# Deferred split subtracts, a LayerNorm scaled by VectorE, later triangle transposes and a merge that starts with two blocks by channels, in a hybrid gMLP, S5 and attention block

## The chip, the cores and the metric

One core of one Trainium2 chip runs the whole block in one launch. The metric is the device time of one execution in microseconds. Engines are called as the profile calls them: PE is TensorE, DVE VectorE, ACT ScalarE, POOL GpSimd, SP the engine that issues most loads.

## The reference

One decoder layer on x of shape (1024, 1024) in float32, with three sub-layers, each between RMSNorms. The part around the change is the first one:

```python
h = rms_norm(x, g_mix_pre)
z_gm, z_s5, z_ga, z_gb = split(h @ w_in)                 # 2048, 512, 1024, 1024 columns
u, v = split(gelu(z_gm))
v = layer_norm(v, ln_g, ln_b)
sv = einsum('gts,bnsgc->bntgc', tril(w_s), v) + b_s      # 8 chunks of 128 positions, 8 channel groups of 128
y_gm = u * sv
y_s5 = s5(z_s5);  y_s5 = y_s5 * sigmoid(y_s5 @ w_glu)    # 512 channels
merged = sigmoid(z_ga) * (y_gm @ w_br_gm) + sigmoid(z_gb) * (y_s5 @ w_br_s5)
x = x + rms_norm(merged @ w_mix_out, g_mix_post)
```

Cross-attention into a memory of 256 positions and a SwiGLU feed-forward layer follow; the change does not touch them.

## The kernel before, in words

**Float32 products from three fast ones.** Every large product is made of operands that are split in two float32r tiles, a high and a low half: `put` (line 527) copies the source to the high half on ScalarE (line 529) and subtracts that from the source on VectorE (line 530). Weights are split the same way by `split` (lines 103 and 104), from a raw tile that SP has loaded (line 94). `mm3` issues three matmuls, high by high, high by low and low by high (all appear at line 519). `tblock` (line 539) makes one 128x512 tile in a PSUM bank, over n channel groups, three products each. There are 8 PSUM banks of 128x512, 38 slots of 128x1024 in SBUF, 8 buffers of split weights and 3 of raw weights.

**Order.** The program is recorded in a fixed order; each engine and each DMA queue works through its instructions in the order in which they are recorded. Side work is written as generators that are put in a queue (`bg`); `sub()` (line 67), called after every second channel group of the main products (6 matmuls), advances each generator that is due and then splits at most one weight tile ahead. A generator's `yield n` puts it off for n calls of `sub`. So the place of a side step among the matmuls is set by these counts. A weight tile is split ahead only while fewer than 7 of the 8 split buffers are in use and at most 3 tiles ahead; `rel` gives buffers back. A raw weight load stands in SP's queue behind the subtract of an earlier split, whose buffer it takes, and the other loads of SP behind it.

**The stages around the change**, in this order:

1. `v_phase` (line 1146) makes v in two halves of four 128x1024 tiles, from products in the four banks X and the four banks Y. For one half of the positions, `ln` (line 1153) gets the mean from sums that the GELUs accumulated, the variance from squares on ScalarE (line 1160), then a reciprocal root in ten small VectorE operations (`rms_slow`), and normalizes: one small VectorE product for the bias (line 1164) and one ScalarE activation with scale and bias for each of four tiles (line 1167). `ln(1)` runs beside the product "21" into Y; after it come the adds that empty Y (line 1247) and their GELUs, and then the product "T4" into X, whose GELUs (line 1255) are followed by `ln(0)`. The generator `wturn` (line 1218), put in the queue ahead of "T4", transposes the triangular position weights on TensorE (line 1223), in two groups of four tiles, copies them out on ScalarE (line 1224), and adds to the bias tile a product with the LayerNorm's bias (lines 1230 and 1231), again in two groups. The first transposes take the first bank that line 1247 has emptied.
2. `s5_out` (line 1060) makes the GLU: for each of 4 channel blocks m and each half of the positions, 12 matmuls, a sigmoid on ScalarE (line 1076), a multiply on VectorE (line 1077) and the split `put` (line 1078). The next product, with `w_br_s5`, needs all four blocks as channels: its first two output blocks are made as four tiles, over channels 0 to 2 first and then over channel 3; the other six follow with `tblock`. Each tile is multiplied out of PSUM by the gate `gb` on VectorE and stored by ScalarE's DMA queue (`mb`).
3. `gm_gen` (line 1259) runs as side work among these products, the gating: for each of 8 channel groups and each half, four matmuls of v with the triangle into one bank, `scalar_tensor_tensor` out of PSUM (line 1282, seen at line 140), a multiply by u (line 1284, seen at line 134) and `put` (line 1285), one half at every second `sub`. u is loaded by SP one group ahead (line 1267).
4. `merge` (line 1291) drains the side work, then makes eight output blocks of two halves each: 24 matmuls over the eight channel groups with `w_br_gm`, multiplied by `ga` (line 1311), added to `mb` (line 1312) and split. `ga` and `mb` of the next block are loaded ahead (lines 1297 and 1298).

Of the kernel before, what the change touches and what calls it, by code (L numbers as in the profile page):

```python
# [9 lines left out]
F = mybir.dt.float32  # L10
# [26 lines left out]
class Builder:  # L37
# [1022 lines left out]
    def s5_out(self):  # L1060
        nc = self.nc
        while len(self.yT) < 4 or not self.yok:
            self.sub()
        yT, self.yT = self.yT, None
        yr, self.yr = self.yr, None
        ys = []
        for m in range(4):
            if m % 2 == 0:
                w = self.get(("glu", m // 2))
            y = self.pair()  # L1070
            t = self.slot()
            for half in range(2):
                o = slice(half * 512, half * 512 + 512)
                ps = self.bank()
                self.tblock(ps, w, (m % 2) * 128, lambda k: tuple(s[:, o] for s in yT[k]), 4)
                nc.scalar.activation(out=t[:, o], in_=ps, func=AF.Sigmoid)  # L1076
                self.tt(t[:, o], t[:, o], yr[m][:, o], ALU.mult)
                self.put(tuple(s[:, o] for s in y), t[:, o])
            ys.append(y)
            if m % 2:  # L1080
                self.rel()
        yT = yr = None
        gb = {}

        def lg(m):
            gb[m] = self.slot()
            nc.sync.dma_start(gb[m], self.gd["gb"][m])
        lg(0)
        lg(1)
        self.bg(self.gm_gen(), 3)  # L1090
        late = []
        w = self.get(("bs", 0))

        tiles = [(m, half, self.bank()) for m in range(2) for half in range(2)]
        for ks in (range(3), range(3, 4)):
            for m, half, ps in tiles:
                for k in ks:
                    self.mm3(ps, tuple(x[:, k, m * 128:m * 128 + 128] for x in w),
                             tuple(s[:, half * 512:half * 512 + 512] for s in ys[k]), k == 0, k == 3)
                self.sub()  # L1100
                if ks[0]:
                    o = slice(half * 512, half * 512 + 512)
                    self.tt(gb[m][:, o], ps, gb[m][:, o], ALU.mult)
        tiles = ps = None
        self.rel()
        late += [(self.gd["mb"][m], gb.pop(m)) for m in range(2)]
        lg(2)
        for m in range(2, 8):
            if m < 7:
                lg(m + 1)  # L1110
            if m % 2 == 0:
                w = self.get(("bs", m // 2))
            g = gb.pop(m)
            for half in range(2):
                o = slice(half * 512, half * 512 + 512)
                ps = self.bank()
                self.tblock(ps, w, (m % 2) * 128, lambda k: tuple(s[:, o] for s in ys[k]), 4)
                self.tt(g[:, o], ps, g[:, o], ALU.mult)
            if m % 2:
                self.rel()  # L1120
            while late:
                nc.scalar.dma_start(*late.pop(0))
            late.append((self.gd["mb"][m], g))
        nc.scalar.dma_start(*late.pop(0))
# [21 lines left out]
    def v_phase(self, fin):  # L1146
# [6 lines left out]
        def ln(half):  # L1153
            st = sums[half]
            mu = st[:, 40:44]
            self.tt(mu, st[:, 32:36], st[:, 36:40], ALU.add)
            self.ts(mu, mu, -1.0 / D, ALU.mult)
            for t in range(4):
                j = self.jk.tile([P, 1024], BF, name="jk", tag="jk", bufs=1)
                nc.scalar.activation(out=j, in_=vt[4 * half + t], func=AF.Square, bias=mu[:, t:t + 1],  # L1160
                                     accum_out=st[:, t:t + 1])
                yield 1
            yield from self.rms_slow(st, 4)
            self.tt(st[:, 48:52], mu, st[:, 16:20], ALU.mult)
            for t in range(4):
                v = vt[4 * half + t]
                nc.scalar.activation(out=v, in_=v, func=AF.Identity, scale=st[:, 16 + t:17 + t], bias=st[:, 48 + t:49 + t])  # L1167
                if t % 2:
                    yield 1
            if not half:  # L1170
                self.vok = True
# [75 lines left out]
            self.tt(vt[t][:, h0], Y[t], vt[t][:, h0], ALU.add)  # L1247
            gelu(vt[t][:, h0], vt[t][:, h0], st(0, 0, t))
        Y = None
        self.bg(wturn(), 2)  # L1250
        run(X, "T4", False)
        del self.fxs["T4"]
        self.hT = None
# [5 lines left out]
    def gm_gen(self):  # L1259
        nc, i = self.nc, self.ins  # L1260
        self.ygm = [None] * 8
        us = {}

        def lu(g):
            if g < 8:
                us[g] = self.slot()
                nc.sync.dma_start(us[g], self.ud[g])
        lu(0)
        while not self.vok:
            self.sub()  # L1270
        for g in range(8):
            y = self.pair()
            lu(g + 1)
            u = us.pop(g)
            for half in range(2):
                o = slice(half * 512, half * 512 + 512)
                ps = self.bank()
                for n in range(4):
                    self.mm(ps[:, n * 128:n * 128 + 128], self.vt[4 * half + n][:, g * 128:g * 128 + 128],
                            self.wt[:, g * 128:g * 128 + 128], True, True)  # L1280
                t = self.tmp()
                self.stt(t.rearrange("p (n t) -> p n t", n=4), ps.rearrange("p (n t) -> p n t", n=4), self.gc[:, 32 + g:33 + g],
                         self.bb[:, g * 128:g * 128 + 128].unsqueeze(1).to_broadcast([P, 4, 128]), ALU.mult, ALU.add)
                self.tt(u[:, o], t, u[:, o], ALU.mult)
                self.put(tuple(s[:, o] for s in y), u[:, o])
                yield 2
            self.ygm[g] = y
            u = y = t = ps = None
        self.vt = self.bb = None

    def merge(self):
# [3 lines left out]
        def lg(m):  # L1295
            ld[m] = (self.slot(), self.slot())
            nc.sync.dma_start(ld[m][0], self.gd["ga"][m])
            nc.sync.dma_start(ld[m][1], self.gd["mb"][m])
        self.drain()
        lg(0)  # L1300
        self.mg = self.halves()
        for m in range(8):
            if m < 7:
                lg(m + 1)
            w = self.get(("a", m))
            g, b = ld.pop(m)
            for half in range(2):
                o = slice(half * 512, half * 512 + 512)
                ps = self.bank()
                self.tblock(ps, w, 0, lambda k: tuple(s[:, o] for s in self.ygm[k]))  # L1310
                self.tt(g[:, o], ps, g[:, o], ALU.mult)
                self.tt(g[:, o], g[:, o], b[:, o], ALU.add)
                self.put(self.hv(self.mg, half, m, True), g[:, o])
                if half:
                    self.rel()
        self.ygm = self.wt = None
# [647 lines left out]
```

## Time and profile before

| | |
|---|---|
| median of 3 runs | 1670.89 us (1670.71 to 1671.16) |
| the profiled execution's own time | 1670.15 us |
| its span, first to last instruction | 1668.4 us |
| TensorE busy, mean granted clock | 1628.1 us (98%), 0.994 |
| VectorE, ScalarE busy | 1150.6 us (69%), 681.7 us (41%) |

Times in the profile count from the span's start. A row's line number is often that of a helper: 519 is every split product, 134, 140 and 146 are the VectorE helpers `tt`, `stt` and two-operation `ts`, 144 is `ts` with one operation, 529 and 530 are `put`. Matmul ends are modelled, and a few matmul records can be missing, so counts of a stretch can be one or two short.

### The profile page before, as it was taken

What the parts mean: (1) busy time and instruction counts of PE and PEld (TensorE: products, weight loads), DVE (VectorE), ACT (ScalarE), POOL (GpSimd) and SP (SyncE); (2) the same over time, 40 slices, a digit from 0 to 9 for tenths busy, and PEclk for the clock granted to TensorE, in tenths of its full rate; (3) what the DMA queues carried; (4) which work ended last, traced back from release to release, by engine and by line L of the source; (5) the groups of instructions that cost most, each with busy time, mean ns of one, the idle gap of its engine ahead of it and who ended that gap; (6) DMA issues with size and microseconds to landing.
All of it is one profiled execution on the core that took longest, in us unless ns stands there. A gap on an engine that the chain in (4) does not pass through costs nothing.

```text
span 1668.4 us, 20995 instructions
## 1 busy us (share of the span) xinstructions
PE 1628.1 (98%) x7788; PEld 1364.4 (82%) x7788; DVE 1150.6 (69%) x2053; ACT 681.7 (41%) x1196; POOL 102.7 (6%) x97
## 2 busy tenths in 40 slices
PE   7999989999999999999999999999999999999997
PEld 7898878887887778888888888888888888888886
DVE  5679788967444674447864577687778777666778
ACT  6642212135457222235543447753233223245454
POOL 0025500012500000000000000000000000000000
PEclk9999999999999999999999999999999999999999
DMA  8669922245231474444523153673545446463634
GB/s 278 207 122 200 234 74 90 76 134 186 113 113 51 163 283 158 141 147 143 172 69 125 53 192 112 216 244 130 180 139 173 149 158 202 142 225 132 226 112 161
DMA packets 223414, 259.53 MB, mean 156 GB/s; under 512 B 14824, under 2 KB 157200, under 8 KB 223120
## 3 DMA queue, kind: packets, MB, share of 16 engines
q1 hardware_dynamic: 176208, 181.24, 33.7%
q10 hardware_dynamic: 26496, 60.18, 9.7%
q0 software_dynamic: 20608, 16.78, 5.9%
q8 instruction: 61, 1.00, 0.2%
q14 instruction: 41, 0.34, 0.1%
HBM read 183.31 MB, written 77.33 MB: 156 GB/s over the span
## 4 chain that ended last, share of the span: by engine, by line
PE 83%; DVE 7%; ACT 5%; issue 2%; DMA 2%; SPq 0%; ACTq 0%; DVEq 0%
PE ps L519 79%; DVE act L134 2%; DVE ws L104 1%; ACT jk L575 1%; DVE ws L134 1%; ACT ws L103 1%; DMA wr<-in_ca_w_kv_dram 1%; ACT act L529 1%; DVE act L530 1%; DVE act L140 1%; PE ps L587 1%; ACT jk L1160 1%; DMA wr<-actd 1%; PE ps L508 1%; ACT act L1167 0%
## 5 line engine op out<-in xcount | busy, mean ns | idle before, releaser
L519 PE MATMUL ps<-act,ws 128*128 128x512 f32 (+1 forms) x4212 | 970.1, 388 | 9.6 <-ACT act L529 7.3
L519 PEld LDWEIGHTS ps<-act,ws 128*128 128x128 f32 x4212 | 775.4, 189 | 165.9 <-ACT act L529 8.1
L519 PE MATMUL ps<-ws,act 128*128 128x512 f32 x1392 | 332.8, 395 | 0.0
L519 PEld LDWEIGHTS ps<-ws,act 128*128 128x128 f32 x1392 | 270.2, 208 | 45.0
L134 DVE TENSOR_TENSOR act<-act 128x512 f32<-128x512 f32 (+6 forms) x521 | 287.3, 580 | 15.2 <-ACT act L1076 8.0
L519 PE MATMUL ps<-ws 128*128 128x512 f32 x852 | 193.3, 389 | 0.0
L519 PEld LDWEIGHTS ps<-ws 128*128 128x128 f32 x852 | 159.9, 188 | 33.2
L104 DVE TENSOR_TENSOR ws<-wr,ws 128x1024 fp32r<-128x1024 f32 x100 | 122.1, 1223 | 93.3 <-ACT ws L103 93.1
L134 DVE TENSOR_TENSOR act<-ps,act 128x512 f32<-128x512 f32 x201 | 135.6, 683 | 43.5 <-PE ps L519 34.1
L134 DVE TENSOR_TENSOR ws<-act,ws 128x512 fp32r<-128x512 f32 x107 | 74.0, 692 | 88.9 <-ACT ws L1754 51.8
L134 DVE TENSOR_TENSOR ws<-tm,ws 128x512 fp32r<-128x512 f32 x108 | 78.2, 724 | 79.4 <-ACT ws L1547 58.9
L1547 ACT CAST ws<-tm 128x512 fp32r<-128x512 f32 x88 | 54.8, 622 | 168.8 <-PE ps L519 111.5
L103 ACT CAST ws<-wr 128x1024 fp32r<-128x1024 f32 x100 | 104.7, 1047 | 42.8 <-PE ps L519 29.3
L134 DVE TENSOR_TENSOR ws<-wr,ws 128x512 fp32r<-128x512 f32 x130 | 91.7, 706 | 28.2 <-ACT ws L1547 14.9
L529 ACT CAST act<-act 128x512 fp32r<-128x512 f32 (+1 forms) x92 | 57.5, 637 | 129.5 <-DVE act L134 117.1
L530 DVE TENSOR_TENSOR act<-act 128x512 fp32r<-128x512 f32 (+1 forms) x92 | 65.3, 720 | 46.1 <-ACT act L529 46.1
L519 PE MATMUL ps<-act 128*128 128x256 f32 (+2 forms) x504 | 86.6, 317 | 0.2
L519 PEld LDWEIGHTS ps<-act 128*128 128x128 f32 x504 | 74.7, 190 | 9.6 <-DVE act L134 0.8
L1754 ACT CAST ws<-act 128x512 fp32r<-128x512 f32 x71 | 44.2, 622 | 89.6 <-PE ps L519 48.3
L1831 POOL DMA_DIRECT2D out_dram<-act x4 | 2.2, 561 | 1171.8 <-DVE act L134 1171.8
L530 DVE TENSOR_TENSOR act<-ps,act 128x512 fp32r<-128x512 f32 x48 | 32.5, 687 | 39.7 <-ACT act L529 39.7
L890 ACT ACTIVATE act<-ps 128x512 f32<-128x512 f32 x32 | 19.2, 600 | 80.4 <-PE ps L519 46.6
(164 smaller groups left out, 1112.5 us busy)
## 6 DMA issues: line engine op xcount, KB each, us to landing
wr<-in_ffn_w_gu_dram SPq DMA_DIRECT2D x39, 512.0 KB, 4.2
actd<-act ACTq DMA_DIRECT2D x77, 256.0 KB, 2.2
wr<-actd SPq DMA_DIRECT2D x38, 512.0 KB, 3.7
wr<-in_w_in_dram SPq DMA_DIRECT2D x28, 512.0 KB, 3.9
act<-in_ffn_w_gu_dram SPq DMA_DIRECT2D x22, 512.0 KB, 5.1
act<-in_ffn_w_down_dram SPq DMA_DIRECT2D x44, 256.0 KB, 4.3
td<-act POOLq DMA_DIRECT2D x40, 256.0 KB, 6.6
pd<-act ACTq DMA_DIRECT2D x17, 512.0 KB, 4.4
```

Source lines behind the costliest of these rows:

```text
L103: self.nc.scalar.copy(hi, t)
L104: self.nc.vector.tensor_tensor(out=lo, in0=t, in1=hi.bitcast(F), op=ALU.subtract)
L134: self.nc.vector.tensor_tensor(out=out, in0=a, in1=b, op=op)
L140: self.nc.vector.scalar_tensor_tensor(out=out, in0=a, scalar=s, in1=b, op0=op0, op1=op1)
L508: nc.tensor.matmul(py[:, o], self.rr[:, 512 + i * 128:640 + i * 128], cc[:, 512 + i * 128:640 + i * 128], start=False, stop=True)
L519: self.nc.tensor.matmul(ps, a, b, start=start, stop=stop, skip_group_check=more)
L529: self.nc.scalar.copy(dst[0], src)
L530: self.nc.vector.tensor_tensor(out=dst[1], in0=src, in1=dst[0].bitcast(F), op=ALU.subtract)
L575: self.nc.scalar.activation(out=j[:, 0:n], in_=src, func=AF.Square, accum_out=col)
L890: nc.scalar.activation(out=g[:, half * 512:half * 512 + 512], in_=ps, func=AF.Sigmoid)
L1547: self.nc.scalar.copy(t[:, 0:512], now)
L1754: nc.scalar.copy(w[:, h[0]], src)
```

## The change

It has four parts.

- In `s5_out` and in `gm_gen` the split's ScalarE copy is recorded where it was, and its VectorE subtract one half later: behind the multiply of the next half, the last one after the loop (`rest`).
- In `ln` the four normalizations of a half are done by VectorE, one `tensor_scalar` each with two scalars from a statistics tile: add the negative mean, multiply by the reciprocal root. The small product for the bias is gone.
- `wturn` is put in the queue with a delay of 5 instead of 2, so all its four steps come three calls of `sub` later.
- In `merge` the first two blocks are made as four tiles, over channel groups 0 to 5 first, then over groups 6 and 7 of each; `ga` and `mb` of blocks 0 and 1 are loaded at the start, those of block 2 after these tiles, and the split weights of both blocks are given back after them. Blocks 2 to 7 are as before.

```diff
@@ s5_out
+                nc.scalar.copy(y[0][:, o], t[:, o])
+                if rest:
+                    self.tt(*rest, ALU.subtract)
+                rest = y[1][:, o], t[:, o], y[0][:, o].bitcast(F)
-                self.put(tuple(s[:, o] for s in y), t[:, o])
...
+        self.tt(*rest, ALU.subtract)
@@ v_phase, ln
-            self.tt(st[:, 48:52], mu, st[:, 16:20], ALU.mult)
             for t in range(4):
                 v = vt[4 * half + t]
-                nc.scalar.activation(out=v, in_=v, func=AF.Identity, scale=st[:, 16 + t:17 + t], bias=st[:, 48 + t:49 + t])
+                self.ts(v, v, st[:, 40 + t:41 + t], ALU.add, st[:, 16 + t:17 + t], ALU.mult)
@@ v_phase
-        self.bg(wturn(), 2)
+        self.bg(wturn(), 5)
@@ gm_gen
-                self.put(tuple(s[:, o] for s in y), u[:, o])
+                nc.scalar.copy(y[0][:, o], u[:, o])
+                if rest:
+                    self.tt(*rest, ALU.subtract)
+                rest = y[1][:, o], u[:, o], y[0][:, o].bitcast(F)
                 yield 2
...
+        self.tt(*rest, ALU.subtract)
@@ merge
+        lg(1)
+        ws = [self.get(("a", m)) for m in range(2)]
+        tiles = [(m, half, self.bank()) for m in range(2) for half in range(2)]
+        for ks in (range(6), range(6, 8)):
+            for m, half, ps in tiles:
+                for k in ks:
+                    self.mm3(ps, (ws[m][0][:, k], ws[m][1][:, k]),
+                             tuple(s[:, half * 512:half * 512 + 512] for s in self.ygm[k]), k == 0, k == 7)
+                    if k % 2:
+                        self.sub()
+                if ks[0]:
+                    out(m, half, ps)
+            if ks[0]:
+                self.rel()
+                self.rel()
+        lg(2)
-        for m in range(8):
+        for m in range(2, 8):
             if m < 7:
                 lg(m + 1)
+            del ld[m - 2]
```

`out(m, half, ps)` holds the two VectorE operations and the split that stood in the loop before (lines 1311 to 1313).

## Rows read from the trace of the kernel before

**Rows 1.** The page's first part: busy time, share of the span and instruction count of each engine, whole span.

```profile
PE 1628.1 (98%) x7788; PEld 1364.4 (82%) x7788; DVE 1150.6 (69%) x2053; ACT 681.7 (41%) x1196; POOL 102.7 (6%) x97
```

**Rows 2.** Who waited for whom, 480 to 640 us of the span, those of TensorE: engine, line, releaser; total us, times, longest us.

```profile
PE ps L519 <- ACT act L529: 7.3, 2, 3.7
...
PE ps L1223 <- DVE act L134: 3.3, 1, 3.3
```

**Rows 3.** TensorE in order of time, 480 to 560 us: start us, length us, engine, line, operation, tiles, shapes, count, and in brackets the idle time before and what ended it.

```profile
509.94 0.63 PE L1223 MATMUL ps<-ident,act 128*128 128x128 f32 x4 [3.30 <-DVE act L134]
...
510.32 5.73 PE L519 MATMUL ps<-ws,act 128*128 128x512 f32 x24
...
516.25 3.01 PE L519 MATMUL ps<-ws,act 128*128 128x512 f32 x12
...
526.25 17.94 PE L519 MATMUL ps<-act,ws 128*128 128x512 f32 x78
...
547.75 0.50 PE L519 MATMUL ps<-act,ws 128*128 128x512 f32 x1 [3.56 <-ACT act L529]
...
554.76 1.05 PE L519 MATMUL ps<-act 128*128 128x128 f32 x8
```

**Rows 4.** Four stretches: from:to us, length, then busy time and count of each engine; PEclk is the granted TensorE clock as a share of 2.4 GHz; last the DMA share and GB/s.

```profile
509.94:516.25 6.31, 6.31 (x33) 5.29 (x33) 1.65 (x3) 6.31 (x13) 0.00 (x0) 1.00 0.10 34
...
547.75:554.76 7.01, 6.78 (x21) 5.22 (x22) 4.70 (x8) 4.25 (x7) 0.00 (x0) 0.76 0.65 220
...
563.63:603.53 39.90, 39.90 (x221) 34.53 (x220) 31.55 (x47) 8.63 (x13) 0.00 (x0) 1.00 0.61 222
...
615.33:624.50 9.17, 9.17 (x28) 7.09 (x29) 6.53 (x9) 2.18 (x3) 0.00 (x0) 0.69 0.81 308
```

**Rows 5.** VectorE (DVE) and ScalarE (ACT) in order of time around 509 us and, last, ScalarE at 519 us; columns as in group 3.

```profile
509.03 0.16 DVE L134 TENSOR_TENSOR st<-st 128x4 f32<-128x4 f32 x1
...
509.11 2.48 DVE L134 TENSOR_TENSOR act<-ps,act 128x512 f32<-128x512 f32 x4
...
509.23 4.64 ACT L1167 ACTIVATE act<-act,st 128x1024 f32<-128x1024 f32 x4 [2.75 <-DVE st L134]
...
519.07 0.60 ACT L1186 ACTIVATE act<-ps 128x512 f32<-128x512 f32 x1
```

**Rows 6.** VectorE groups by line and shape over the whole span: tiles, shapes, count, busy us, mean ns of one, idle us before.

```profile
L144 DVE TENSOR_SCALAR act<-act,st 128x1024 f32<-128x1024 f32 x17 | 12.2, 747 | 0.1
...
L140 DVE SCALAR_TENSOR_TENSOR act<-act,st 128x1024 f32<-128x1024 f32 x20 | 25.6, 1279 | 0.2
```

**Rows 7.** The stretch of the glu products (526 to 548 us), VectorE and then ScalarE in order of time; columns as in group 3.

```profile
531.52 0.69 DVE L134 TENSOR_TENSOR act<-act 128x512 f32<-128x512 f32 x1 [1.61 <-ACT act L1076]
...
534.97 0.69 DVE L134 TENSOR_TENSOR act<-act 128x512 f32<-128x512 f32 x1
...
542.90 0.69 DVE L134 TENSOR_TENSOR act<-act 128x512 f32<-128x512 f32 x1 [5.19 <-ACT act L1076]
...
545.22 1.23 DVE L104 TENSOR_TENSOR ws<-wr,ws 128x1024 fp32r<-128x1024 f32 x1 [0.26 <-ACT ws L103]
...
537.74 4.64 ACT L1167 ACTIVATE act<-act,st 128x1024 f32<-128x1024 f32 x4 [1.43 <-DVE st L134]
...
547.08 0.62 ACT L529 CAST act<-act 128x512 fp32r<-128x512 f32 x1 [1.40 <-DVE act L134]
```

**Rows 8.** VectorE in the gating stretch, in order of time; columns as in group 3.

```profile
561.66 0.69 DVE L134 TENSOR_TENSOR act<-tm,act 128x512 f32<-128x512 f32 x1 [5.06 <-DMA act<-ud]
...
582.56 0.68 DVE L134 TENSOR_TENSOR act<-ps,act 128x512 f32<-128x512 f32 x1
...
583.94 0.69 DVE L134 TENSOR_TENSOR act<-tm,act 128x512 f32<-128x512 f32 x1
...
585.31 0.69 DVE L530 TENSOR_TENSOR act<-act 128x512 fp32r<-128x512 f32 x1 [0.69 <-ACT act L529]
...
585.92 0.68 DVE L134 TENSOR_TENSOR act<-ps,act 128x512 f32<-128x512 f32 x1
...
590.77 0.68 DVE L134 TENSOR_TENSOR act<-ps,act 128x512 f32<-128x512 f32 x1
```

**Rows 9.** The start of the merge, in order of time: TensorE's first merge products, ScalarE's copy of the last group's first half, TensorE going on; columns as in group 3.

```profile
606.62 5.02 PE L519 MATMUL ps<-act,ws 128*128 128x512 f32 x21
...
614.66 0.62 ACT L529 CAST act<-act 128x512 fp32r<-128x512 f32 x1 [2.79 <-DVE act L134]
...
615.33 9.88 PE L519 MATMUL ps<-act,ws 128*128 128x512 f32 x30 [3.69 <-ACT act L529]
```

**Rows 10.** VectorE taking merge tiles out of PSUM, in order of time; columns as in group 3.

```profile
624.57 0.69 DVE L134 TENSOR_TENSOR act<-ps,act 128x512 f32<-128x512 f32 x1 [1.01 <-PE ps L519]
...
630.01 0.69 DVE L134 TENSOR_TENSOR act<-ps,act 128x512 f32<-128x512 f32 x1 [1.15 <-PE ps L519]
...
635.45 0.69 DVE L134 TENSOR_TENSOR act<-ps,act 128x512 f32<-128x512 f32 x1 [2.65 <-PE ps L519]
```

**Rows 11.** Loads of the u tiles, 500 to 640 us (tiles, queue, count, KB each, median us from issue to landing), the line of those loads in the view of the tile ud (queue, count, issue ns min/median/max, first and last start us), and the last line of the view of the tile mbd, over the span.

```profile
act<-ud SPq DMA_DIRECT2D x8, 512.0 KB, 5.3
...
L1267 SPq DMA_DIRECT2D act<-ud x8: 320/430/590, 556.3 to 606.3; - x8
...
DMA to landing us min/median/max: 5.6/6.4/9.6
```

More of the change, by code (lines that the diff above doesn't have):

```diff
@@ L1065, in s5_out @@
         yr, self.yr = self.yr, None
-        ys = []
+        ys, rest = [], None
         for m in range(4):
@@ L1081, in s5_out @@
                 self.rel()
-        yT = yr = None
+        self.tt(*rest, ALU.subtract)
+        yT = yr = rest = None
         gb = {}
@@ L1270, in gm_gen @@
             self.sub()
+        rest = None
         for g in range(8):
@@ L1288, in gm_gen @@
             u = y = t = ps = None
+        self.tt(*rest, ALU.subtract)
+        rest = None
         self.vt = self.bb = None
@@ L1301, in merge, with out @@
         self.mg = self.halves()
-        for m in range(8):
+        def out(m, half, ps):
+            g, b = ld[m]
+            o = slice(half * 512, half * 512 + 512)
+            self.tt(g[:, o], ps, g[:, o], ALU.mult)
+            self.tt(g[:, o], g[:, o], b[:, o], ALU.add)
+            self.put(self.hv(self.mg, half, m, True), g[:, o])
+        lg(1)
[13 more added lines that the diff above has]
+                self.rel()
+        ws = tiles = ps = None
+        lg(2)
+        for m in range(2, 8):
             if m < 7:
                 lg(m + 1)
+            del ld[m - 2]
             w = self.get(("a", m))
-            g, b = ld.pop(m)
             for half in range(2):
@@ L1310, in merge @@
                 self.tblock(ps, w, 0, lambda k: tuple(s[:, o] for s in self.ygm[k]))
-                self.tt(g[:, o], ps, g[:, o], ALU.mult)
-                self.tt(g[:, o], g[:, o], b[:, o], ALU.add)
-                self.put(self.hv(self.mg, half, m, True), g[:, o])
+                out(m, half, ps)
                 if half:
```

## The prediction

> **What bounds the kernel now.** First the busy shares: TensorE is busy for 1628.1 of 1668.4 us [rows 1], so only time in which TensorE stands still or runs slowly can be won, and the next view is who TensorE waits for between 480 and 640 us. There are three places. The transposes of line 1223 wait 3.30 us for VectorE; two products of line 519 wait 7.3 us together for the cast of line 529, the ScalarE half of a split [rows 2]. The time line puts them at 506.6 to 509.9 (gap A), 544.2 to 547.75 (gap B) [rows 3] and 611.6 to 615.3 us (gap C) [rows 9]. Third, the granted clock of the stretches behind the gaps: 1.00 (2.4 GHz) behind A, but 0.76 behind B and 0.69 behind C, part of those stretches at the lower level, 1.2 GHz [rows 4]. So B and C cost more than their idle time.
>
> A product's pitch: two merge halves of 24 products each leave PSUM at 630.01 and 635.45, VectorE waiting for TensorE both times [rows 10], so 5.44 / 24 = 0.2267 us. With it the price of each gap:
> - A: 3.3 us; the clock stays at its upper level [rows 4].
> - B: 3.56 idle plus 0.23 for the low half. The 21 products from 547.75 to 554.76 [rows 3] take 7.01 us instead of 21 x 0.2267 = 4.76: 2.25 lost, 0.23 of it that wait. B costs 3.56 + 2.25 = 5.8.
> - C: at 611.64 TensorE had issued 21 of the first half's 24 products [rows 9]. The 27 up to the second half's end would have ended at 611.64 + 6.12 = 617.76; VectorE meets that end at 624.57 [rows 10]. C costs 6.8.
>
> **Gap A, parts one and two.** Why VectorE is late there: the transposes take the first bank that line 1247 empties, and that add stands behind the small operations of the LayerNorm, which end at 509.03 [rows 5]. The change puts four normalizations on VectorE ahead of that add, and lets the transposes come after 5 pump steps of 6 products instead of 2. The norm's price: its form (two scalars from a tile) is not in the trace. Below lies line 144, the same operation with one such scalar, 0.747 us; above, the three-operand form of line 140, 1.279 us [rows 6]. I take the lower end, at a start-to-start pitch of about 0.69, as it has one tensor operand like line 144. The bank is free at 509.03 + 4 x 0.69 + 0.69 = 512.5. TensorE arrives at 506.64 + 18 x 0.2267 = 510.7, so a wait of about 1.8 is left: gain 1.5. At 1.28 the bank would come at 514.8 and the wait be 4.1, longer than now.
>
> The second transposes (0.38, from 509.94 to 510.32 in rows 3) move out of this product into the first glu product; the bias products and their two adds (0.6 each on VectorE) move two halves later. TensorE pays the same for them; on VectorE they matter in B.
>
> **Gap B, parts one and two.** TensorE waits for the split of the third glu channel block's first half, cast at 547.08 [rows 7]. ScalarE is late because it normalizes for 4.64 us at 537.74 while VectorE stands idle 5.19 us [rows 7]. The order is worked forward:
> - The product T4 ends at 512.6 + 0.38 + 18 x 0.2267 = 517.1 instead of 516.25 + 12 x 0.2267 = 518.97 [rows 3], so ScalarE's last GELUs start 1.75 earlier than 519.07 [rows 5], and the chain behind with them: the second half's multiply comes at 529.7 instead of 531.5 [rows 7].
> - VectorE's 128x512 operations follow each other at 2.48 / 4 = 0.61 [rows 5]. Behind it VectorE has the multiply 0.61, the deferred subtract 0.61 (now without waiting for its cast), a bias add 0.61 and eight small rsqrt steps at about 0.19 (0.16 is one's busy time [rows 5]), 1.5: the third half's multiply at 533.0 instead of 534.97. Then multiply, subtract, bias add (1.83), the last rsqrt steps 0.7 and four norms 2.8: the fourth half's multiply at 538.3 instead of 542.90 [rows 7].
> - Cast, a weight split (its subtract was at 545.22 [rows 7], now 540.6), multiply: the fifth half's cast at 542.5, ready at 543.1, 4.6 earlier. Its low half is now recorded behind the sixth half's multiply and ready at 545.0.
> - TensorE arrives at 517.1 + 96 x 0.2267 + 0.38 + 1.6 (two sets of bias products, in shape like the eight at 554.76 [rows 3], 0.8 each with the overlap) + 6 x 0.2267 = 542.2. It waits 0.9 for the cast and, one product later, 1.6 for the low half: 2.5 in place of 3.8. **Here the deferral costs something:** the low half comes later than its cast allows.
>
> TensorE's wait of 3.30 left the clock at its upper level, that of 3.56 did not [rows 3, 4]; each of the two new ones is well under both, so I take the upper level and count the 2.25 - 0.23 = 2.0 as won. B gives 1.3 + 2.0 = 3.3. Lower bound 1.3 (the clock falls all the same), upper bound 5.8 (no wait). The walk gives the gating's first product at 549.5 against 554.76 [rows 3], 5.2 earlier; A and B added give 4.8, the rest being rounding.
>
> **The gating stretch.** TensorE is full at the upper clock there [rows 4], so deferral wins nothing on it directly. What it changes is VectorE's lag. From one PSUM multiply to the next it needs 3.36 us (582.56 to 585.92), and 4.85 with a weight split (585.92 to 590.77) [rows 8], on average 3.7, where TensorE gives a step every 12 x 0.2267 plus 0.8 to 1.05 for its eight small products [rows 3], about 3.6. So VectorE never makes up the 5.06 us for which it awaits the first u tile [rows 8], and is late at the merge. Each step holds 0.69 of waiting for the cast [rows 8]; the deferral takes that out: about 2.7, or 4.7 with a split. It starts 5 us earlier, since the u loads stand in SP's queue behind the weight load that the last glu split releases, and ends about 604, with TensorE leaving the stretch at 606.62 - 5.2 = 601.4.
>
> **Gap C, part three.** The two first blocks now run channels 0 to 5 of all four tiles, 72 products or 16.3 us, before the last two groups. These are asked for at 617.7, over 13 us after they are there; the order alone would cover gap C, and so would nearly the faster gating. C goes entirely: 6.8. What comes due together instead: four tiles leave PSUM in 5.4 us of products but need about 2.7 us each (multiply and add 0.69 each, cast 0.62, subtract 0.69 [rows 7]); with 8 banks and the next two halves of 5.44 that delays no product. The loads of blocks 0 and 1 are both issued at once on SP, ahead of need; the next weight pairs are split only after two releases, four halves, 21.8 us, before their use. Cost nothing, covered by these; without that cover one split, 1.2 us, would show.
>
> **Sum.** 1.5 + 3.3 + 6.8 = 11.6, by the walk 12.0; I take 12. From there to the end TensorE is bound by its products and everything moves along. The profiled execution took 1670.15 us, so 1658.2; the median of the runs is 0.74 above it: 1658.9.
>
> A rule speaks against B. The Trainium skill, "TensorE: Matmul & The Clock Gate", section "A second HAM failure mode: psum-queue depth-cycling", says that short idle times between groups of products, frequent enough, make the clock swing between its levels. By it the clock behind B would stay low; in this trace a single wait of 3.30 us did not lower it, and no run here shows two shorter ones in a row.
>
> **Rivals.**
> - The clock falls behind B all the same. For it: two waits close together, 2.5 us in all; against: the full clock after one wait of 3.30 [rows 4]. 2.0 less: 1660.9. Chance 0.17.
> - The norm costs 1.28 on VectorE. A then waits 4.1, and the fourth glu half comes at about 543 again: A loses 0.8 and B gains nothing, only C and some of the lag is won: about 6 faster, 1665. For it: two scalars read from a tile, not seen here; against: line 144. Chance 0.08.
> - The low halves are in time after all (the weight split falls elsewhere): another 2.5, 1656.4. Chance 0.15.
> - Slower: u tiles loaded too late. The deferred subtract holds a u slot half a step longer, so with the 38 slots nearly full a load may get a slot that a store has just left, and SP, in order, stops behind it. A load that waits for group g's last subtract must land before group g + 2: at 5.3 us plus 0.43 of issue [rows 11] and two VectorE operations of 0.61, a group takes 6.95, within TensorE's 7.26. At the longest landing of a tile here, 9.6 [rows 11], it takes 11.25, so 4 us for each of six groups, 24 less the 12 gained: 1683. It decides from 7.6 us of landing on. Against: the median. Chance 0.04.
> - The change does nothing where it matters, because only the order of records moves and TensorE still meets the same VectorE operation: no change. Against: rows 7 show ScalarE's 4.64 us in the chain. Chance 0.03.
>
> **Numbers.** The forecast itself has 0.53. 0.2% (3.3 us) is about what a measurement of this kernel can tell from no change. All cases but the last two are faster by more than that: 0.93, of which I leave 0.03 to costs not seen; so faster 0.90, same 0.05, slower 0.05. The range reaches from the case without a wait (1656.4, a little under) past the fallen clock towards the slow norm: 1656 to 1664, leaving out most of the slow norm, no change and slower.
>
> **What would show it.** Right: no PE wait at line 1223 over 2 us; line 1167 gone from ScalarE and eight tensor-scalars of 0.75 us at line 144's neighbour 146; at the bs products two waits under 2 us and a granted clock of 1.00 behind; VectorE's subtracts of the gating without a wait for their cast; no wait at the merge's products and 1.00 behind. Wrong: a norm of over 1 us, a clock below 0.9 at the gating's start, VectorE waiting for u loads more than once, or a TensorE wait anywhere in 600 to 640 us.

## The result, and the profile after

The changed kernel takes 1659.64 us (median of 4 runs, 1658.76 to 1660.26) where the kernel before, run beside it, takes 1670.8: a ratio of 0.9935, 95% interval 0.9923 to 0.9946, so 11 us faster. The profiled execution took 1658.76 us with a span of 1657.0.

TensorE in the changed kernel, in order of time (columns as in [rows 3], whose gaps it answers):

```profile
511.46 0.63 PE L1226 MATMUL ps<-ident,act 128*128 128x128 f32 x4 [2.05 <-DVE act L134]
...
542.05 0.51 PE L519 MATMUL ps<-act,ws 128*128 128x512 f32 x1 [0.43 <-ACT act L1078]
543.88 6.46 PE L519 MATMUL ps<-act,ws 128*128 128x512 f32 x20 [1.32 <-DVE act L134]
550.18 1.05 PE L519 MATMUL ps<-act 128*128 128x128 f32 x8
...
601.99 58.29 PE L519 MATMUL ps<-act,ws 128*128 128x512 f32 x256
```

The transposes (now line 1226) wait 2.05 us where they waited 3.30. At the bs products (those with `w_br_s5`) the waits of 3.56 and 0.23 have become two of 0.43 and 1.32: the first for the cast, the second for the low half, whose subtract now stands behind the next multiply. At the merge there is no wait at all: products run on from 601.99, where 3.69 us were lost before [rows 9].

The granted clock of three stretches of the changed kernel (columns as in [rows 4]):

```profile
512.00:516.00 4.00, 4.00 (x19) 3.31 (x19) 2.22 (x3) 4.00 (x10) 0.00 (x0) 1.00 0.00 0
...
544.00:548.00 4.00, 4.00 (x11) 3.19 (x12) 2.94 (x5) 2.48 (x5) 0.00 (x0) 0.59 0.63 239
...
611.00:615.00 4.00, 4.00 (x19) 3.31 (x18) 0.00 (x0) 0.00 (x0) 0.00 (x0) 1.00 1.02 392
```

Behind the transposes and at the merge the clock is at its upper level; behind the bs products it still falls, to 0.59 over 4 us. The products from 543.88 to 550.18 take 6.30 us for 20 x 0.2267 = 4.53, so 1.77 are lost. The same 20 products before, behind the wait of 0.23:

```profile
548.48 6.45 PE L519 MATMUL ps<-act,ws 128*128 128x512 f32 x20 [0.23 <-DVE act L530]
```

From there to the small products at 554.76 [rows 3] they took 6.28 us, so 1.75 were lost. The low clock behind the bs products costs what it cost before.

VectorE in the changed kernel, in order of time: the norms and the add behind them; the fourth half's multiply and the subtract behind it (542.90 before [rows 7]); in the gating two waits for u tiles and four multiplies out of PSUM (answering [rows 8]); the last subtracts.

```profile
507.73 2.98 DVE L146 TENSOR_SCALAR act<-act,st 128x1024 f32<-128x1024 f32 x4
510.63 2.48 DVE L134 TENSOR_TENSOR act<-ps,act 128x512 f32<-128x512 f32 x4
...
537.20 1.29 DVE L134 TENSOR_TENSOR act<-act 128x512 f32<-128x512 f32 x2
...
555.28 0.69 DVE L134 TENSOR_TENSOR act<-tm,act 128x512 f32<-128x512 f32 x1 [3.27 <-DMA act<-ud]
...
587.50 0.69 DVE L134 TENSOR_TENSOR act<-tm,act 128x512 f32<-128x512 f32 x1 [1.26 <-DMA act<-ud]
...
588.71 0.68 DVE L134 TENSOR_TENSOR act<-ps,act 128x512 f32<-128x512 f32 x1
...
593.56 0.68 DVE L134 TENSOR_TENSOR act<-ps,act 128x512 f32<-128x512 f32 x1
...
596.15 0.68 DVE L134 TENSOR_TENSOR act<-ps,act 128x512 f32<-128x512 f32 x1
...
598.73 0.68 DVE L134 TENSOR_TENSOR act<-ps,act 128x512 f32<-128x512 f32 x1
...
603.99 1.47 DVE L134 TENSOR_TENSOR act<-act 128x512 fp32r<-128x512 f32 x2
```

ScalarE's cast of the fifth half in the changed kernel (547.08 before [rows 7]):

```profile
541.38 0.62 ACT L1078 CAST act<-act 128x512 fp32r<-128x512 f32 x1 [1.40 <-DVE act L134]
```

Four norms take 510.63 - 507.73 = 2.90, so 0.725 each. A half step of the gating takes 2.58 us (596.15 to 598.73) where it took 3.36, and 4.85 with a weight split (588.71 to 593.56), as before. VectorE is done with the gating at 605.5, 3.5 us after TensorE has left it.

One caution for all that follows. Ahead of the norm all kernels here run the same instructions in the same order, yet in profiles of kernels that are alike up to the transposes these begin anywhere from 511.46 to 516.17. So times of single executions differ by a few us for reasons outside the change. The table therefore gives the **stretch**: from the end of T4's first 12 products (where the transposes stood before) to the merge's first product. It is read from the time lines: where the transposes come after 30 products, their start less their wait less 18 x 0.2267 is its beginning (30 x 0.2267 where they come after 42, in experiment 11). Gap C lies behind it.

| kernel | wait at transposes | waits at bs products | low clock behind | stretch | wait at merge | ratio to before |
|---|---|---|---|---|---|---|
| before | 3.30 | 3.56 + 0.23 | bs, merge | 99.98 | 3.69 | 1 |
| changed | 2.05 | 0.43 + 1.32 | bs | 96.66 | none | 0.9935 |
| changed, run again | 2.05 | 1.3 | transposes | 96.0 | none | 0.9942 |

The spans of the first two profiles differ by 11.4 us: 1.3 ahead of the stretch (506.64 and 505.33), 3.3 in it and 6.8 in the merge, from its first product to the first behind it (606.62 to 700.53 before, 601.99 to 689.12 in the changed kernel). So 10.1 of the 11.4 lie where the change is.

### The profile page after: what moved, and what is told of

Its sections match the earlier page's. It is cut to its first block, busy times and chain, and to the rows that moved or that the text cites. A ratio compares the mean times of both kernels' runs of the same rounds, so it can differ in the third digit from the quotient of the medians.

```text
span 1657.0 us, 20995 instructions
## 1 busy us (share of the span) xinstructions
PE 1624.1 (98%) x7788; PEld 1362.3 (82%) x7788; DVE 1153.2 (70%) x2059; ACT 672.4 (41%) x1188; POOL 103.2 (6%) x97
## 4 chain that ended last, share of the span: by engine, by line
PE 81%; DVE 9%; ACT 5%; DMA 3%; issue 2%; ACTq 1%; SPq 0%; DVEq 0%
PE ps L519 77%; DVE act L134 3%; DVE ws L104 1%; ACT ws L103 1%; DMA wr<-in_ca_w_kv_dram 1%; DVE ws L134 1%; DVE act L140 1%; ACT jk L575 1%; PE ps L587 1%; ACT jk L1164 1%; DMA wr<-actd 1%; DVE st L140 1%; PE ps L508 0%; ACTq L453 0%; DVE act L486 0%
## 5 line engine op out<-in xcount | busy, mean ns | idle before, releaser
L134 DVE TENSOR_TENSOR act<-act 128x512 f32<-128x512 f32 (+6 forms) x545 | 303.4, 585 | 14.5 <-ACT act L1076 7.2
L529 ACT CAST act<-act 128x512 fp32r<-128x512 f32 (+1 forms) x68 | 42.6, 644 | 72.0 <-DVE act L134 69.1
L530 DVE TENSOR_TENSOR act<-act 128x512 fp32r<-128x512 f32 (+1 forms) x68 | 48.8, 730 | 29.5 <-ACT act L529 29.5
```

The costliest lines, as they stand in the source:

```text
L134: self.nc.vector.tensor_tensor(out=out, in0=a, in1=b, op=op)
L529: self.nc.scalar.copy(dst[0], src)
L530: self.nc.vector.tensor_tensor(out=dst[1], in0=src, in1=dst[0].bitcast(F), op=ALU.subtract)
```

## The experiments

Each was timed in 5 rounds beside the kernel before. Diffs are against the changed kernel where nothing else is said.

**1. The merge as before.** The first two blocks are made by `tblock` again.

```diff
-        for ks in (range(6), range(6, 8)):
-            for m, half, ps in tiles:
...
-        for m in range(2, 8):
+        for m in range(8):
```

> The changed kernel with the merge's first two blocks as they were, the other three parts kept. Theory: VectorE has made up its lag by the end of the gating, because the deferred subtracts no longer wait for their casts, so the last group's split is there (low half of its first half at about 605) when TensorE asks for it (21 products behind the merge's start, about 606.7). No TensorE wait at the merge, the time is that of the changed kernel, 1659.6 within 1 us. Rival: the new order of the merge is what covers gap C; then a wait of some 3.7 us and the fallen clock come back, 6.8 us, 1666.4.

Measured: 1659.59 us, ratio 0.9927 (0.9915 to 0.9939), stretch 96.6. Its waits in the stretch are the changed kernel's, and there is none at the merge. The rows are VectorE's last subtracts of the gating and the weight split behind them:

```profile
605.31 1.46 DVE L134 TENSOR_TENSOR act<-act 128x512 fp32r<-128x512 f32 x2
607.03 1.23 DVE L104 TENSOR_TENSOR ws<-wr,ws 128x1024 fp32r<-128x1024 f32 x1 [0.26 <-ACT ws L103]
```

The merge's first product came at 603.31 there, so the last group's first half is asked for at 603.31 + 21 x 0.2267 = 608.1; its low half is the first of the two subtracts at 605.31, done at about 606.0. With the other parts there, the merge's new order adds nothing.

**2. The merge and the gating as before**, so without the gating's deferral too.

```diff
-                nc.scalar.copy(y[0][:, o], u[:, o])
-                if rest:
-                    self.tt(*rest, ALU.subtract)
-                rest = y[1][:, o], u[:, o], y[0][:, o].bitcast(F)
+                self.put(tuple(s[:, o] for s in y), u[:, o])
...
-        self.tt(*rest, ALU.subtract)
```

> As the run with the merge as before, and the gating's subtracts again directly behind their casts; norm on VectorE, glu's deferral and later triangles kept. Theory: VectorE needs 3.4 to 4.9 us for a half step again and ends the gating about 10 us later than in the changed kernel, so TensorE waits about 5.5 us for the last group at the merge and the clock falls behind it: 6.8 to 8 us over the changed kernel, 1666.5 to 1667.6. Rival: the earlier start of the gating (some 5 us) is enough by itself for the last group; then 1659.6.

Measured: 1666.27 us, ratio 0.9964 (0.9952 to 0.9977), 6.7 over the run of experiment 1 beside it. Gap C is back, with a wait of 3.7 where about 5.5 was expected. TensorE's waits in this kernel (as in [rows 2]):

```profile
PE ps L519 <- ACT act L529: 3.7, 1, 3.7
PE ps L1226 <- DVE act L134: 2.0, 1, 2.0
PE ps L519 <- DVE act L134: 1.3, 1, 1.3
```

The granted clock in it behind the transposes, at the bs products and behind the merge's wait (columns as in [rows 4]):

```profile
512.00:516.00 4.00, 3.51 (x11) 2.90 (x12) 2.23 (x5) 3.62 (x10) 0.00 (x0) 0.61 0.00 0
...
544.00:548.00 4.00, 2.68 (x12) 1.91 (x11) 2.60 (x5) 2.48 (x6) 0.00 (x0) 1.00 0.99 335
...
611.00:615.00 4.00, 3.37 (x8) 2.48 (x9) 2.90 (x5) 1.26 (x3) 0.00 (x0) 0.60 1.02 418
```

So without the merge's new order it is the gating's deferral that removes gap C; the earlier start of the gating alone does not. The second reading was not expected: here the clock fell behind the 2.05 us at the transposes and stayed up at the bs products. But the waits there are not the changed kernel's. Behind the transposes 18 products took 5.77 us (512.90 to 518.67) where they took 4.20 in the changed kernel (511.84 to 516.04). TensorE therefore reached the bs products later, found the cast done, and only the wait of 1.3 for the low half is left.

**3. The norm on ScalarE**, the other parts kept.

```diff
+            self.tt(st[:, 48:52], mu, st[:, 16:20], ALU.mult)
...
-                self.ts(v, v, st[:, 40 + t:41 + t], ALU.add, st[:, 16 + t:17 + t], ALU.mult)
+                nc.scalar.activation(out=v, in_=v, func=AF.Identity, scale=st[:, 16 + t:17 + t], bias=st[:, 48 + t:49 + t])
```

> The changed kernel with the LayerNorm's normalization back on ScalarE (and its small bias product), the other parts kept. Theory: the transposes then wait for nothing, since the adds that empty the banks come at once (2 us won), but ScalarE's 4.6 us at the glu come back and the bs products wait some 6 to 8 us in all: the gating starts about 3.7 us later, and the end comes 3.7 us later, 1663.3, up to 1 more if the clock stays low longer. Rival: the deferred subtracts alone free the chain at the glu and the norm's place does not matter there: 1657.6, faster than the changed kernel by the 2 us of the transposes.

Measured: 1664.74 us, ratio 0.9955 (0.9943 to 0.9968), 5.1 slower than the changed kernel and 5.2 than experiment 1 beside it; the stretch is 101.5. The transposes wait for nothing; the bs products wait 7.0 us:

```profile
PE ps L519 <- DVE act L134: 4.2, 2, 3.2
PE ps L519 <- ACT act L1078: 2.8, 1, 2.8
```

and the clock behind is 0.50 from 548 to 556 us:

```profile
548.00:552.00 4.00, 2.54 (x5) 1.75 (x6) 2.84 (x5) 2.48 (x5) 0.00 (x0) 0.50 0.91 303
552.00:556.00 4.00, 4.00 (x11) 3.04 (x11) 3.08 (x5) 2.19 (x4) 0.00 (x0) 0.50 0.24 92
```

The norm's place is what moves gap B; the deferred subtracts and the later triangles without it do not.

**4. Two channels first at the bs products.**

```diff
-        for ks in (range(3), range(3, 4)):
+        for ks in (range(2), range(2, 4)):
```

> The changed kernel with the first four bs tiles made over channels 0 and 1 first and then over 2 and 3, where it had 0 to 2 and then 3. TensorE then has 24 products before it needs the third channel block in place of 6. Theory: the two waits of 0.4 and 1.3 us go, at most 0.8 us is left at the fourth channel, and the clock behind stays at its upper level: 1.8 of waits less and 1.8 of the lower clock less, about 3 us under the changed kernel, 1656 to 1657. Rival: the clock falls behind this stretch for the sake of the earlier waits (the transposes' 2.0 us) or of the small products, so that only the waits go: 1658. Second rival: the third block's waits only move to the fourth, nothing is won: 1659.6.

Measured: 1660.13 us, ratio 0.9928 (0.9915 to 0.9942): not the 3 us. The waits of TensorE's products at the bs products are gone and the clock stays at 1.00:

```profile
544.00:548.00 4.00, 4.00 (x23) 3.45 (x22) 2.59 (x4) 2.48 (x6) 0.00 (x0) 1.00 0.99 344
```

But a new chain takes their place. VectorE waits for the first u tile, and TensorE, whose banks VectorE should empty, waits behind it. VectorE's wait in this kernel:

```profile
560.00 0.69 DVE L134 TENSOR_TENSOR act<-tm,act 128x512 f32<-128x512 f32 x1 [7.49 <-DMA act<-ud]
```

TensorE's two waits for VectorE in this kernel:

```profile
561.41 1.65 PE L519 MATMUL ps<-act,ws 128*128 128x512 f32 x6 [1.52 <-DVE tm L140]
563.34 1.16 PE L519 MATMUL ps<-act 128*128 128x128 f32 x8 [0.28 <-DVE act L134]
```

The stretch is 95.4, 1.2 shorter than the changed kernel's: 1.75 of waits and about 1.8 of clock are won, 1.8 of bank waits are new, and about half a us goes to a weight load that waits 0.53 for the last low half.

The late u tile is not a matter of order alone. Its load was issued 45.0 us into the stretch (552.35), as in the changed kernel (550.34), but was awaited until 560.00, 7.6 us later, where it took 4.9 there. Estimated from these two, a load of 4.9 us would have left none of the 1.8. Whether the other executions had such a load too is open: their median is no lower.

**5. The glu's split at once**, the gating's deferral kept.

```diff
-                nc.scalar.copy(y[0][:, o], t[:, o])
-                if rest:
-                    self.tt(*rest, ALU.subtract)
-                rest = y[1][:, o], t[:, o], y[0][:, o].bitcast(F)
+                self.put(tuple(s[:, o] for s in y), t[:, o])
...
-        self.tt(*rest, ALU.subtract)
```

> The changed kernel with the glu's subtracts again directly behind their casts (gating's deferral, norm, triangles and merge kept). Theory: the cast of the third block's first half then comes some 1.5 us later, since VectorE waits for each cast before the next multiply, but its low half follows at once; TensorE waits once, about 2.5 us and 0.5, where the changed kernel has 0.4 and 1.3. From the first transposes to the merge's first product about 91 us against 90.5 in the changed kernel; time 1660 within 1. Rival, from the prediction's remark that the deferral costs the low half's wait: without it that 1.3 us goes and nothing comes in its place, 89.2 us, 1658.3.

Measured: 1661.06 us, ratio 0.9935 (0.9922 to 0.9948), stretch 97.0. One wait of 2.0 for the cast and one of 0.2 for the low half, 2.2 in place of 1.75:

```profile
PE ps L519 <- ACT act L529: 2.0, 1, 2.0
PE ps L519 <- DVE act L530: 0.2, 1, 0.2
```

The low half's wait has shrunk by 1.1 and the cast's has grown by 1.5: the deferral of the glu is worth about half a us of waits, below what these timings resolve. The clock fell behind these waits too, to 0.61 from 548 to 552 us.

**6. The triangles as before.**

```diff
-        self.bg(wturn(), 5)
+        self.bg(wturn(), 2)
```

> The changed kernel with the triangles' transposes 2 calls into T4 as before, the rest kept. Theory: VectorE's four norms now stand ahead of the bank that the transposes take, so TensorE waits 2.05 + 3 x 6 x 0.2267 = 6.1 us there instead of 2.05, and gets about 1 back at the bs products, where it then arrives later: 3 us slower, 1662.6, and up to 2 more with the clock falling behind so long a wait, 1664.7. Rival: TensorE was early at the bs products anyway, and all of it is given back there: 1659.6.

Measured: 1665.11 us, ratio 0.9955 (0.994 to 0.9969), a little over the expected 1662.6 to 1664.7. TensorE waits 6.1 us at the transposes, the clock is 0.50 from 512 to 516 us, and nothing waits at the bs products any more:

```profile
512.00:516.00 4.00, 2.78 (x9) 2.42 (x10) 2.87 (x5) 2.89 (x9) 0.00 (x0) 0.50 0.00 0
...
PE ps L1226 <- DVE act L134: 6.1, 1, 6.1
```

The stretch of its profile is 98.1, only 1.4 over the changed kernel's, since TensorE then arrives late at everything else; that execution (1661.35) is the shortest of its six, and why the others are up to 5 us longer is open.

**7. The norm alone**, against the kernel before.

> The kernel before with the norm by VectorE alone. Theory: the wait of gap A grows from 3.3 to 6 us, that of gap B shrinks from 3.8 to about 2, the lower clock is paid once behind A in place of B, and gap C stays, since VectorE's half step of the gating is as long as before: no change, 1671 within 2. Rival: the norm's 4.6 us on ScalarE was the cause of B and C both, so that the norm alone brings the most of the gain: 1662 to 1664.

Measured: 1674.37 us, ratio 1.0015 (1.0006 to 1.0024): the expected no change, 1671 within 2, was missed by a little, for it is 2.5 us slower. The stretch of its profile is 101.2 against 99.98, the clock 0.50 from 512 to 516 us, in and behind the first of its waits:

```profile
PE ps L1222 <- DVE act L134: 6.1, 1, 6.1
PE ps L519 <- ACT act L529: 3.7, 1, 3.7
PE ps L519 <- DVE act L134: 1.0, 1, 1.0
PE ps L519 <- DVE tm L140: 0.8, 1, 0.8
```

What the bs products no longer wait, the transposes do, and gap C (the 3.7) stays; the last two rows are waits for banks in the gating (566.9 to 570.4 us), new here. The part that decides gap B gains nothing without the later triangles and the gating's deferral.

**8. The merge alone**, against the kernel before.

> The kernel before with the merge's new order alone. Theory: the order covers the whole of gap C by itself, whoever is late, since the last two groups are asked for 16 us later; with gaps A and B as before that is 6.8 us, 1664.3 within 1.5. With the run that had the merge as before and was as fast as the changed kernel, this would show that either of the two, the order or the gating's deferral, removes gap C, and only once. Rival: VectorE's lag goes on into the merge and the four tiles that end together make TensorE wait at the third block; then 1667 or more.

Measured: 1666.86 us, ratio 0.9968 (0.9955 to 0.998), stretch 99.9. Waits of 3.30 at the transposes and 3.6 at the bs products as before, none at the merge, the clock there 1.00:

```profile
PE ps L519 <- ACT act L529: 3.6, 1, 3.6
PE ps L1223 <- DVE act L134: 3.3, 1, 3.3
...
613.00:625.00 12.00, 12.00 (x54) 9.95 (x53) 7.21 (x10) 2.19 (x3) 0.00 (x0) 1.00 0.83 319
```

The time misses the expected 1664.3 within 1.5 by 1.1: it is 4.7 under the median beside it, where 6.8 was expected (its interval reaches from 3.3 to 7.5). The profile has the 6.8: from the merge's first product to the first behind the merge are 87.1 us (607.69 to 694.83) against 93.9 before. Why the median gained less is open. With experiments 1 and 2: the order of the merge removes gap C on the kernel before, the gating's deferral removes it beside the norm and the later triangles, and it can be removed once.

**9. Two channels first, the first u tiles early.** As experiment 4, with the first two u tiles loaded at the start of `s5_out`.

```diff
+        self.us = {}
+        for g in range(2):
+            self.us[g] = self.slot()
+            nc.sync.dma_start(self.us[g], self.ud[g])
...
-        for ks in (range(3), range(3, 4)):
+        for ks in (range(2), range(2, 4)):
...
```

> The changed kernel with two channels first at the bs products (as in the run before) and the first two u tiles loaded ahead of the glu. In the run with two channels first the waits at the bs products were gone and the clock stayed up, but VectorE then waited 7.5 us for the first u tile and TensorE 1.8 us for banks behind it. Theory: with u there, that goes too; from the first transposes to the merge's first product 87.5 us against 90.5 in the changed kernel and 89.3 in that run; time 1656.5 to 1657.5. Rival: the early loads only crowd out the weight loads on SP and the glu waits for weights instead: 1660 or more.

Measured: 1660.17 us, ratio 0.9928 (0.9914 to 0.9942). The median misses the expected 1656.5 to 1657.5, but its profiled execution took 1655.75. There the stretch is 93.1, 3.5 under the changed kernel's, with one wait of TensorE's products left in it, the clock at 1.00 throughout:

```profile
PE ps L1230 <- DVE act L134: 2.0, 1, 2.0
```

**10. The changed kernel again, and experiment 9 again**, side by side.

> The changed kernel itself, on the same chip and in the same rounds as the two runs with two channels first. Both theories: 1659.6 within 1. If the clock falls by chance in this stretch, its profile may show it behind the transposes, behind the bs products or nowhere; the waits themselves (2.05, 0.4, 1.3) should be the same.

> Two channels first and early u tiles, a second time. In the first run the profiled execution was 3.0 us under the changed kernel's and had no wait in the stretch but the transposes' 2.05, yet the median was 1660.2. Theory: the stretch is 3 us shorter in most executions and the median of the first run was held up by work elsewhere or by the chip; then 2 to 3 us under the changed kernel run beside it. Rival: the other executions lose these 3 us again inside the stretch, by the clock falling behind the transposes; then the median is that of the changed kernel, and a profile that shows it has a clock under 0.7 behind the transposes.

Measured: the changed kernel 1661.92 us, ratio 0.9942 (0.9929 to 0.9954), over the expected 1659.6 within 1; the other 1657.22 us, 0.9921 (0.9909 to 0.9934), stretch 93.1 again. So 4.7 us between the medians of this pair, of which the profiles place 2.9 in the stretch (96.0 against 93.1); the rest is open. The other's profiled execution is the slowest of its five (1659.83), but not by the stretch: its transposes begin only at 516.17, where those of the first began at 512.07. In the changed kernel's second profile the clock fell behind the transposes, and not at the bs products. As in experiment 2 only one wait is left there:

```profile
PE ps L1226 <- DVE act L134: 2.0, 1, 2.0
PE ps L519 <- DVE act L134: 1.3, 1, 1.3
...
516.00:520.00 4.00, 4.00 (x12) 3.17 (x11) 2.09 (x3) 4.00 (x10) 0.00 (x0) 0.60 0.00 0
544.00:548.00 4.00, 3.31 (x15) 2.30 (x13) 3.14 (x5) 1.85 (x4) 0.00 (x0) 1.00 0.28 83
```

**11. Experiment 9 with the transposes after 7 calls.**

```diff
-        self.bg(wturn(), 5)
+        self.bg(wturn(), 7)
```

> The changed kernel with two channels first, the first two u tiles early, and the transposes 7 calls into T4 where the change has 5. Theory: TensorE arrives at the transposes 2 x 6 x 0.2267 = 2.7 us later and no longer waits the 2.05 there, but then reaches the bs products 2 us earlier and waits up to 1.9 us there for the second channel block, so that little is won by time; what it can win is the clock, which in these runs fell behind the transposes or behind the bs products in some executions: 0 to 2 us under the run without the delay. Rival: the second wait is covered too, 2 us faster for certain.

Measured: 1657.93 us, ratio 0.9923 (0.9909 to 0.9936). The wait at the transposes is gone and comes back as 1.9 us for VectorE at the bs products (1.6 and 0.3, some 5 us apart); the stretch is 93.2, practically the same. The clock stayed up, as in the two profiles without the delay.

```profile
PE ps L519 <- DVE act L134: 1.9, 2, 1.6
```

## Why the prediction was right, step by step

The forecast was 12 us and 1658.9; measured were 11.2 us and 1659.64. That the two numbers lie so close is in part luck. The parts were summed to 11.6, and the profiles place 10.1 where the change is. 1.3 of their difference lies ahead of the change, where both kernels run the same instructions, and the changed kernel run again was 9.6 under the kernel beside it.

- **Gap A**: forecast a wait of about 1.8, gain 1.5; measured 2.05, gain 1.25. The norm costs 0.725 where 0.69 was taken; nearly everything else of the chain held. The rival price of 1.28 is out.
- **Gap B, idle**: forecast 2.5 left of 3.8; measured 1.75, gain 2.0 where 1.3 was counted. The fifth half's cast comes 5.7 us earlier than before, 4.4 of it against the same point of T4, where 4.6 was forecast. (By the prediction's own times T4 ends 518.97 - 517.1 = 1.9 earlier, not the 1.75 that it carried on; 0.1 us.)
- **Gap B, clock: the one step that failed.** It said that waits well under 3.30 us leave the clock up, since that of 3.30 did. In the changed kernel's profile the clock fell behind 0.43 and 1.32, and of the 2.0 us counted as won nothing came: 1.77 lost against 1.75 before. (The 2.0 also held some 0.27 that was not clock: the record of the single product ahead of the 20 is 0.50 long, not 0.2267.) The rival that says so had a chance of 0.17.

  The step was wrong as a way of reading, not only in this case: behind the same 2.05 us at the transposes the clock fell in experiment 2 and in the changed kernel's second profile and stayed up in six others of these profiles, while behind 3.30 it stayed up both times that it was seen. A single wait's length did not order these cases.

  What the rival named, two waits close together, fits better at the bs products: the clock fell all five times that exactly two waits stood there, one product apart (before and experiment 8: 3.56 and 0.23; changed kernel and experiment 1: 0.43 and 1.32; experiment 5: 1.97 and 0.23), fell among the three of experiment 3, and stayed up both times that only that of 1.3 was left. That is seen after the fact and in few cases, and no run was made to test it; what decides is open.

  The Trainium skill's rule ("TensorE: Matmul & The Clock Gate", section "A second HAM failure mode: psum-queue depth-cycling"), which was held against the step, agrees with the five, as far as two waits in a row count as frequent. It speaks of repeated idle times, not of single ones, behind which the clock fell twice at the transposes.
- **Gap C**: forecast 6.8, all of it; measured so (6.8 in the profiles, before against the changed kernel and against experiment 8; between experiments 1 and 2 it is 6.7 by the medians and 6.0 in the merge of their profiles). The prediction said that the order alone would cover it and the faster gating nearly so. The order alone does, wholly; the faster gating does, with 2.1 us to spare in experiment 1, but was run only beside the norm and the later triangles. VectorE's half step of 2.7 came out at 2.58, the end of the gating at 605.5, or 606.8 counted as before, where 604 was forecast: 4.85 with a split, not 4.7, and one more wait of 1.26 us for a u tile.
- **Slower, by late u tiles**: TensorE lost nothing to them in the changed kernel, though one load landed only after 7.7 us and VectorE waited twice, 3.27 and 1.26. Only in experiment 4 did such a load cost TensorE time, 1.8 us. The rival's limit of 7.6 us of landing was worked out wrong: by its own terms it is 7.26 - 0.43 - 2 x 0.61 = 5.6, near the 5.3 of the median, so the case was less far off than it says.
- **The low halves**: the remark that the deferral costs something at the glu is half right. The wait for the low half is there (1.32), but without the deferral the cast's wait grows by more (experiment 5).
- **The signs that were named**: two of those for wrong came, a clock below 0.9 at the gating's start and VectorE waiting for u loads more than once; and the wait at the transposes is just over the 2 us named for right. The first is the failed step, the second cost TensorE nothing.

The parts' worth, one taken from the whole: norm about 5 us (5.1 by the medians, 4.9 in the stretch), later triangles 1.4 in the stretch of the one profile and 3 to 5 by the times (ratios 0.9955 and 0.9935, medians 5.5 apart), gating's deferral and merge together 6.7, the merge alone nothing, the glu's deferral unresolved. The gating's deferral was not taken out with the merge's new order in place; that it would cost nothing there is argued from experiment 8. The norm alone, on the kernel before, is worth less than nothing. The parts don't add: each moves a wait to where another part takes it off.

## What to carry to other kernels

Where engines work through fixed orders, walk the two or three queues forward from one known time with durations from the trace; that gave the waits to within a us. What the clock does behind a wait is another matter: one wait behind which it stayed up is no ground for counting it as up behind shorter ones. When a wait has two possible covers, test each alone, for its gain comes only once. And take the next thing that is late (here the first u tile) along with the wait that is removed, or it takes its place.

## What the runs showed of the hardware that was not expected

- The granted clock fell to about 0.6 over 4 us behind single waits of 2.05 us at the transposes in two profiles of eight, and cost about 1.6 us each time; in two profiles of the same kernel it fell at different places. The loss is not all added: TensorE then came to the bs products 1.6 us later, one wait and the fall there were gone, and the stretch was even a little shorter (96.0 and 96.3 against 96.7 and 96.6).
- A `tensor_scalar` with two scalars from a tile, 128x1024 in float32, takes 0.725 us from start to start, close to the 0.747 busy of the one-scalar form [rows 6].
- Loads of one size from the same place in the same queue order land at different times: the first of three u tiles issued in a row was used 4.9 us after its issue in the changed kernel, 5.4 before (556.31 to 561.66), 6.2 in experiments 1 and 6 and 7.6 (552.35 to 560.0) in experiment 4. Two gate loads follow in the queue each time; the cause is open.
